# A fused attention and mixture-of-experts layer: another order of attention work, and bias table and count moved to the last experts

## The chip, the cores and the metric

The kernel runs on one core of a Trainium2 chip. The metric is the device time of one execution in microseconds (us). All arithmetic on data is in 32-bit floats, in parts of the attention as a sum of a rounded high part and a low part.

## The reference, cut to what matters

```
mod = split(silu(c) @ w_ada + b_ada, 6)
h   = modulate(rms_norm(x), mod[0], mod[1])            # hc likewise from the context
out_a = windowed_gqa(qa, ka, va, ka_c, va_c, sink)     # 8 heads, scores, softmax, values
out_b = mla_latent(qn, qr, kn, kr, vb, ...)            # 8 heads, scores, softmax, values
y   = concat(out_a, out_b) @ w_o
x   = x + mod[2] * rms_norm(y)
h2  = modulate(rms_norm(x), mod[3], mod[4])
logits = h2 @ w_router + b_router;  top 4 of 32, softmax of the four
for each expert e: f += weight * (swiglu(h2 @ w_gate_up[e] + b_gate_up[e]) @ w_down[e] + b_down[e])
x   = x + mod[5] * rms_norm(f)
```

There are 256 tokens and 256 context tokens of width 1024, 32 experts with an inner width of 1024.

## The kernel before

**Stages.** A first stage loads the first part of the ada weights, normalizes and projects. A second stage, the list of calls from line 751 on, does what is left of the keys and queries, the attention of both head groups, the output projection and the rest of the ada sums. A short stage after it (`XSEQ`) adds the residual, computes the router's logits and picks the experts. Then 32 experts run one after the other, and `finish` scales and writes the output. In the second stage and after it SP, PE, VectorE, ScalarE and GpSimd each run their instructions in the order of the program: the calls are a schedule written out by hand.

**Expert weights.** Each expert has 12 tiles of 128 x 2048 floats (1 MB each): 0 to 3 and 4 to 7 for the two halves of gate and up, 8 to 11 for down. `load` (line 730) sends them on SP's queue, each into one of 18 slots in the fixed order `RSEQ` (line 31): `d0` to `d2` are buffers of the projections, `r` the three buffers of the ring `slot`, `k0`, `q0`, `b0`, `k1`, `q1`, `b1` buffers of the latent keys and queries, `w` two wide buffers that the output weights use before, `x` four more. A slot is filled again when PE has used its tile.

**Ada sums.** The last four of the six parts of `mod` are not computed on PE. `ada_load` (line 410) loads two rows of weights into a tile; at the first tile of a part it also clears the sum on GpSimd and loads the bias. `ada_do` (line 421) adds the tile, scaled, to the part's sum with two VectorE instructions. `ada(1)` (line 742) loads the next tile, if one is left, and then sums the oldest tile. Twelve tiles go through the ring `slot`, which has three buffers; the first two are loaded ahead (lines 751 and 752), then `v_split` (line 561) takes the third buffer, and keeps it until `v_up(3)` (line 566) has used it. So the load of an `ada(1)` waits for the buffer, and SP, which issues it, with it. `spread1` (line 599) sums a part over the partitions with products by ones and multiplies it with a row of gains, `spread0` (line 594) fetches that row on ScalarE's queue, `column` (line 609) turns a part into columns.

**Attention.** `k_mid` and `k_flip` copy and transpose the latent keys of one tile of tokens, `q_up` and `q_flip` those of the queries, `v_up` makes the values. `top_b(h)` (line 631) computes a head's scores once to find its maxima; `shift(g)` (line 638) negates the maxima of a group, transposes them on PE and copies them out; `weights(u)` (line 660) computes two heads' scores again, transposed, and takes exponentials; `values(u)` (line 701) multiplies by the values and divides by the sums; `mix(k)` (line 720) adds a pair of heads' share of the output projection, with the weights that `load_wo` (line 580) has loaded.

**Experts.** In the loop of line 1146, `G_` does half of a gate-and-up product, `T_` transposes its result and computes the activation, `D_` half of the down product; `take` gathers the tokens of the next pair of experts, `place` makes the matrix that puts an expert's rows back, `scatter` adds them to four accumulators `acc`. `first(t)` (line 1073) starts these accumulators with the weighted `b_down` table, which line 1081 fetches on ScalarE's queue. `count` (line 1096) counts the experts with more than 64 tokens; the count is read after `finish`, and decides whether a loop for the rest runs.

Of the kernel before, what the change touches and what calls it, by code (L numbers as in the profile page):

```python
# [7 lines left out]
F32 = mybir.dt.float32  # L8
# [10 lines left out]
P = 128  # L19
D = 1024  # L20
KD = D // P
T = 256
NT = T // P
E = 32
# [46 lines left out]
def layer_kernel(ctx, tc, x, cx, cc, wadr, bada, grows, win0, winB, winC, winD, wuqa, wuqb, wukv, wo, wr, wexp, bgu, bgx, bdn, cols, rows, consts, out):  # L71
# [93 lines left out]
    def pmm(shape=(P, 512)):  # L165
        return ps.tile(list(shape), F32, name="mm", tag="mm", bufs=4)
# [240 lines left out]
    ada_n = [0]  # L407
# [119 lines left out]
    def k_mid(i):  # L527
        k96[i] = pqa.tile([P, 8, 96], F32, name="k96", tag="ct", bufs=2)
        S.copy(k96[i][:, :, 0:64], pk[i].rearrange("p (h d) -> p h d", h=8))
        S.copy(k96[i][:, :, 64:96], krt[:, i][:, None].to_broadcast([P, 8, 32]))  # L530

    def k_flip(i):
        for g in range(2):
            pt = ptp((96, 4, P))
            for j in range(4):
                PE.transpose(pt[:, j], k96[i][:, g * 4 + j], ident)
            ks = slice(i * P, (i + 1) * P)
            split(kTm[0][g][0:96, :, ks], kTm[1][g][0:96, :, ks], pt)
# [31 lines left out]
    y = []  # L570
# [9 lines left out]
    def load_wo(i):  # L580
        w = wide()
        nc.sync.dma_start(w, wo[i])
        for k in range(2):
            wov[2 * i + k] = w[:, k * 1024:(k + 1) * 1024]
# [11 lines left out]
        S.dma_start(gs_[ch], bass.AP(tensor=grows.tensor, offset=grows.offset + (0 if ch == 0 else 1) * D,  # L596
                                             ap=[[0, P], [1, D]]))

    def spread1(ch):
        a, gs = accs[ch], gs_[ch]  # L600
        for n in range(2):
            sl = slice(n * 512, (n + 1) * 512)
            p_ = pmm((P, 512))
            PE.matmul(p_, ones_f, a[:, sl], start=True, stop=True)
            V.tensor_tensor(a[:, sl], p_, gs[:, sl], op=ALU.mult)
# [29 lines left out]
            PE.matmul(s_, qTm[n][0:96, 0, t, j], kTm[0][n][0:96, j], start=True, stop=True)  # L635
            V.tensor_reduce(mxs[n][:, t, j:j + 1], s_, axis=AX.X, op=ALU.max)

    def shift(g):

        m = mxs[g]  # L640
        if g == "a":
            m4 = m.rearrange("p t (h c) -> p t h c", h=2)[:, :, :, 0:4]
            V.scalar_tensor_tensor(m4, m4, -1.0, nsink.rearrange("p (h j) -> p h j", h=2)[:, None].to_broadcast([P, NT, 2, 4]),
                                   op0=ALU.mult, op1=ALU.min)
        else:
            V.tensor_scalar(m[:, :, 0:4], m[:, :, 0:4], -1.0, None, op0=ALU.mult)
        p_ = pmm((P, T))
        for t in range(NT):
            PE.transpose(p_[:, t * P:(t + 1) * P], m[:, t], ident)
        r = rows_[g] = av.tile([P, T], F32R, name="nmax", tag="nmax", bufs=2)  # L650
        S.copy(r, p_)
        if g == "a":
            for h in range(2):
                ess[h] = av.tile([P, T], F32, name=f"es{h}")
                S.activation(ess[h], r.bitcast(F32), AF.Exp, scale=A_SCALE, bias=col[:, G_SINK + h:G_SINK + h + 1])
# [4 lines left out]
    def weights(u):  # L660

        a = u < 4
        pT_[u] = [av.tile([P, 4, T], F32, name="pT", bufs=4) for h in range(2)]
        for g in range(2):
            st = [pmm((P, 2, T)) for h in range(2)]
            for kk in range(2):
                kt = 2 * g + kk
                ks = slice(kt * P, (kt + 1) * P)
                ops = []
                for h in range(2):  # L670
                    if a:
                        k_ = [x_[HALF[h], ks] for x_ in kTg]
                        q_ = [x_[HALF[h], :, u] for x_ in qTg]
                        sl, r = sel[HALF[h], u], rows_["a"][HALF[h]]
                    else:
                        n, j = divmod(2 * (u - 4) + h, 4)
                        k_ = [x_[n][0:96, j, ks] for x_ in kTm]
                        q_ = [qTm[n][0:96, i, :, j] for i in range(2)]
                        sl, r = sel[0:96, j], rows_[n][0:96]
                    ops.append([(k_[0], q_[0]), (k_[0], q_[1]), (k_[1], q_[0]), (sl, r)])  # L680
                for i in range(4):
                    for h in range(2):
                        PE.matmul(st[h][:, kk], *ops[h][i], start=(kk == 0 and i == 0), stop=(i == 3 and not (a and g)),
                                  skip_group_check=True)
                if a and g:
                    t = 3 - kt
                    for c in range(2):
                        for h in range(2):
                            PE.matmul(st[h][:, kk, t * P + c * 64:t * P + c * 64 + 64], mask_s[HALF[h], t, c],
                                      ident_b[HALF[h], HALF[h]], start=False, stop=True, skip_group_check=True)  # L690
            for h in range(2):
                S.activation(pT_[u][h][:, 2 * g:2 * g + 2], st[h], AF.Exp, scale=A_SCALE if a else B_SCALE)  # L692
        adds(u)
# [36 lines left out]
    def load(e, js):  # L730
        for j in js:
            q = RSEQ[len(slots) % len(RSEQ)]
            if q in "rw":
                w = slot() if q == "r" else wide()
            elif q == "x":
                w = rings2[0].tile([P, 2048], F32, name="slot2", tag="slot2")
            else:
                w = (cst if q in tag else p2).tile([P, 2048], F32, name="slot2", tag=tag.get(q, q))
            slots[e, j] = w
            nc.sync.dma_start(w, wexp[e * SLOTS + j])  # L740

    def ada(n):
        for _ in range(n):
            if ada_n[0] < 16:
                ada_load()
            if ada_q:
                ada_do()
# [4 lines left out]
    ada_load()  # L752
    v_split()
    k_mid(2)
    k_mid(3)
    shift("a")
    weights(0)
    k_flip(2)
    k_mid(0)
    weights(1)  # L760
    k_flip(3)
    k_mid(1)
    values(0)
    k_flip(0)
    q_up(0, 0)
    v_up(0)
    ada(1)
# [16 lines left out]
    load_wo(0)  # L784
    q_flip(1, 1)
    load_wo(1)
    ada(1)
    load(0, range(0, 3))
    top_b(0)
    open_y()  # L790
    mix(0)
    values(3)
    top_b(1)
    spread0(0)
    top_b(2)
    top_b(3)
    ada(1)
    mix(1)
    load_wo(2)
    shift(0)  # L800
    top_b(4)
    top_b(5)
    mix(2)
    column(1)
    weights(4)
    ada(1)
    top_b(6)
    top_b(7)
    mix(3)
    load_wo(3)  # L810
    ada(1)
    router_bias()
    spread1(0)
    shift(1)
    weights(5)
    ada(1)
    values(4)
# [1 line left out]
    weights(6)  # L819
    mix(4)  # L820
    ada(1)
    column(2)
    values(5)
    spread0(3)
    ada(1)
    load(0, range(3, 6))
    weights(7)
    mix(5)
    ada(1)
    values(6)  # L830
    load(0, range(6, 8))
    load(1, range(0, 1))
    ada(1)
    mix(6)
    assert ada_n[0] == 16 and not ada_q
    values(7)
    spread1(3)
    mix(KD - 1)
    st2.close()
    stB.close()  # L840
# [204 lines left out]
        V.tensor_tensor(sg, zg, sg, op=ALU.mult)  # L1045
        V.scalar_tensor_tensor(actT[:, 4 * c:4 * c + 4], zl, 1.0, sg, op0=ALU.add, op1=ALU.mult)  # L1046

    def scatter(y, ctt, last=False):
        for t in range(NT):
            for n in range(2):  # L1050
                PE.matmul(acc[t][n], ctt[HALF[n], t], y[HALF[n]], start=False, stop=last, skip_group_check=True)  # L1051

    def act_tile():
        return mo.tile([P, KD, CAP], F32, name="actT")
# [14 lines left out]
        g, i = gs2[e]  # L1069
        return lambda k: g.x[:, k, i]  # L1070

    def first(t):
        px = px_tile().rearrange("p k c -> p (k c)")
        PE.transpose(px[0:E, 0:P], wtok[t], ident)
        wT = mo.tile([E, P], F32, name="wT")
        V.tensor_copy(wT, px[0:E, 0:P])
        for n in range(2):
            PE.matmul(acc[t][n], wT, bd[:, n * 512:(n + 1) * 512], start=True, stop=False, skip_group_check=True)

    bd = mo.tile([E, D], F32, name="bd", tag="xg")  # L1080
    S.dma_start(bd, bdn)
    g0 = pre(0, V, oh0)
    pxs = [acc[0][g].rearrange("p (k c) -> p k c", c=P) for g in range(2)]
    for g in range(2):
# [58 lines left out]
    for e in range(E):  # L1143
        loads(12 * e + 12)
        nxt = e + 1 < E
        if e == 0:
            G_(0, 1, LOW)
            T_(0, 0)
            G_(0, 1, HIGH)
            G_(1, 0, LOW)  # L1150
            T_(0, 1)
            G_(1, 0, HIGH)
            D_(0, LOW)
            T_(1, 0)
            D_(0, HIGH)
            for i in range(2):
                g0.place(i)
            for t in range(NT):
                first(t)
            count()  # L1160
            continue
        g = gs2[e][0] if e % 2 == 0 else pre((e + 1) // 2) if nxt else None
        step = [g.place, g.place] if e % 2 == 0 else [g.take, g.take] if nxt else None
        if step:
            step[0](0)
        G_(e, 1, LOW)
        if step:
            step[1](1)
        if e:
            scatter(ys.pop(e - 1), gs2[e - 1][0].ctt[gs2[e - 1][1]])  # L1170
        G_(e, 1, HIGH)
        if nxt:
            G_(e + 1, 0, LOW)
        T_(e, 1)
        if nxt:
            G_(e + 1, 0, HIGH)
        D_(e, LOW)
        if nxt:
            T_(e + 1, 0)
        D_(e, HIGH)  # L1180
    scatter(ys.pop(E - 1), gs2[E - 1][0].ctt[1], True)

    def finish():
        ssy = [sm.tile([P, 2], F32, name="ssy") for t in range(NT)]
# [186 lines left out]
```

## Time and profile before

| | |
|---|---|
| three runs | 1194.08, 1198.37, 1199.73 us (median 1198.37) |
| profiled execution | 1202.73 us, span 1200.9 us, mean granted clock 0.978 |
| PE busy | 1108.5 us, 92% of the span |
| VectorE, ScalarE, GpSimd busy | 304.6, 231.9, 129.9 us |
| DMA | 446.58 MB, mean 372 GB/s |

The span runs from the first to the last instruction of the profiled execution. PE's busy time counts products that are stretched by waits and by a lower clock, so 92% does not say that PE is the limit. SPq and ACTq are the queues on which SP and ScalarE issue transfers; a transfer's issue is an instruction, its landing comes later. A mean over the span mixes stages: the DMA engines are idle in parts of the attention and never in the experts.

### The profile page before, as it was taken

To read this page: it belongs to the slowest core of one execution; us is meant where nothing else is said; L and a number is where in the kernel's file an instruction comes from. 1 tells how busy PE (TensorE), PEld (TensorE's weight loads), DVE (VectorE), ACT (ScalarE), POOL (GpSimd) and SP (SyncE) were. 2 spreads that over 40 slices of the span, in tenths; PEclk is the share of its full clock that TensorE was granted. 3 is DMA by queue.
4 is the path that set the end of the run, shared out by engine and by line. 5 is a ranking of instruction groups with operands and counts; after the bars stand their busy time and mean duration, and the time that the engine had idled before them with its cause. 6 is when DMAs were issued, how large, how long until landed. Compare 5 with 4: busy or idle time off the path is not lost. (4 is left out here: it accounts for less than half of the span.)

```text
span 1200.9 us, 13600 instructions
## 1 busy us (share of the span) xinstructions
PE 1108.5 (92%) x5441; PEld 476.4 (40%) x5441; DVE 304.6 (25%) x651; ACT 231.9 (19%) x509; POOL 129.9 (11%) x186
## 2 busy tenths in 40 slices
PE   7699999999999999999999899999998999999885
PEld 2588756553343434343333333333333333333321
DVE  3876566742111121211111111111111111111112
ACT  3533612131111111121111111111111111111101
POOL 0301313310101010101101010101010101010000
PEclk9889998998999999999999999999999999999998
DMA  9740182899999999999999999999999999999994
GB/s 379 289 163 31 36 352 103 324 412 422 419 421 420 421 419 420 419 420 420 421 420 421 420 420 421 420 421 420 420 420 421 420 420 420 421 420 421 420 421 176
DMA packets 63194, 446.58 MB, mean 372 GB/s; under 512 B 7284, under 2 KB 7540, under 8 KB 10008
## 3 DMA queue, kind: packets, MB, share of 16 engines
q1 hardware_dynamic: 62648, 444.24, 89.7%
q10 hardware_dynamic: 480, 1.44, 0.4%
q8 instruction: 44, 0.72, 0.2%
q14 instruction: 22, 0.18, 0.0%
HBM read 444.60 MB, written 1.05 MB: 371 GB/s over the span
## 5 line engine op out<-in xcount | busy, mean ns | idle before, releaser
L1021 PE MATMUL pw<-slot,xg 128*64 128x512 f32 x2048 | 467.5, 598 | 21.0 <-DMA slot<-in_wexp 21.0
L1021 PE MATMUL pw<-slot,actT 128*64 128x512 f32 x1024 | 242.8, 601 | 29.2 <-DMA slot<-in_wexp 28.0
L1021 PEld LDWEIGHTS pw<-slot,xg 128*64 128x64 f32 x2048 | 136.6, 136 | 303.4 <-issue 237.4
L1039 DVE TENSOR_TENSOR z<-pf,bg 128x512 f32<-128x512 f32 x64 | 44.3, 692 | 756.8 <-PE pf L1034 756.8
L1021 PEld LDWEIGHTS pw<-slot,actT 128*64 128x64 f32 x1024 | 68.6, 136 | 179.6 <-issue 103.3
L1043 ACT ACTIVATE sg<-z 128x256 f32<-128x256 f32 x64 | 26.7, 417 | 312.2 <-DVE z L1041 312.2
L1028 ACT COPY gu<-pw 128x512 f32<-128x512 f32 x64 | 37.5, 586 | 229.4 <-PE pw L1021 229.4
L988 PEld LDWEIGHTS px<-oh,xt 128*128 128x128 f32 x480 | 57.2, 195 | 23.9 <-issue 23.9
L1051 PE MATMUL acc<-y,ctt 64*128 64x512 f32 x256 | 63.6, 615 | 0.7 <-ACT y L1028 0.7
L988 PE MATMUL px<-oh,xt 128*128 128x128 f32 x480 | 62.9, 285 | 0.3 <-DVE cnt L1106 0.3
L1000 ACT ACTIVATE xg<-px,vcol 128x128 f32<-128x128 f32 x120 | 45.2, 457 | 92.0 <-PE px L988 92.0
L1034 PEld LDWEIGHTS pf<-con,gu 128*128 128x128 f32 x256 | 26.8, 140 | 52.7 <-issue 51.1
L1034 PE MATMUL pf<-con,gu 128*128 128x128 f32 x256 | 42.0, 286 | 0.7 <-ACT gu L1028 0.7
L1028 ACT COPY y<-pw 128x512 f32<-128x512 f32 x32 | 18.8, 587 | 92.6 <-PE pw L1021 92.6
L723 PE MATMUL y<-slot,of 128*128 128x512 f32 x64 | 32.4, 651 | 2.5 <-DVE of L718 2.3
L978 POOL TENSOR_SCALAR oh<-con,posm,r 128x64 f32<-128x64 f32 x60 | 34.0, 586 | 2.5 <-DVE posm L918 2.5
L1045 DVE TENSOR_TENSOR sg<-z,sg 128x256 f32<-128x256 f32 x64 | 27.2, 425 | 18.0 <-ACT sg L1043 18.0
L1051 PEld LDWEIGHTS acc<-y,ctt 64*128 64x128 f32 x256 | 22.0, 186 | 21.8 <-issue 18.4
L698 POOL TENSOR_TENSOR pa<-pT 128x512 f32<-128x512 f32 x16 | 21.6, 1348 | 70.7 <-ACT pT L692 59.9
L1046 DVE SCALAR_TENSOR_TENSOR actT<-z,sg 128x256 f32<-128x256 f32 x64 | 27.2, 425 | 2.2
L274 PE MATMUL mm<-slot,siluz 128*4 128x512 f32 x40 | 20.0, 653 | 7.5 <-DMA slot<-in_wadr 7.5
L124 POOL TENSOR_TENSOR rstd<-rstd,mh 128x1 f32<-128x1 f32 x14 | 10.7, 766 | 136.9 <-DVE rstd L121 132.9
(449 smaller groups left out, 874.0 us busy)
## 6 DMA issues: line engine op xcount, KB each, us to landing
slot<-in_wexp SPq DMA_DIRECT2D x384, 1024.0 KB, 19.9
slot<-in_wadr SPq DMA_DIRECT2D x20, 1024.0 KB, 8.4
ax<-in_wadr SPq DMA_DIRECT2D x4, 1024.0 KB, 5.8
slot<-in_wo SPq DMA_DIRECT2D x4, 1024.0 KB, 4.8
slot<-in_win SPq DMA_DIRECT2D x2, 1024.0 KB, 8.5
slot<-in_winD SPq DMA_DIRECT2D x2, 768.0 KB, 9.7
slot<-in_winB SPq DMA_DIRECT2D x2, 576.0 KB, 4.8
ct<-in_cx SPq DMA_DIRECT2D x2, 512.0 KB, 8.5
```

The source lines that it names most:

```text
L723: PE.matmul(y[t][n], oT[k][:, t * P:(t + 1) * P], wov[k][:, n * 512:(n + 1) * 512], start=(k == 0), stop=(k == KD - 1), skip_group_check=True)
L978: eng.tensor_scalar(oh[t][:, i], iota[:, 0:CAP], pos_ap(t), r2[t], op0=ALU.is_equal, op1=ALU.mult)
L988: PE.matmul(px[:, k, 0:ne * CAP], xt[t][:, kk * P:(kk + 1) * P], self.oh[t][:, 0:ne].rearrange("p e c -> p (e c)"), start=(k == 0 and t == ...
L1000: S.activation(o, i, AF.Identity, scale=vcol[:, 1, kk:kk + 1], bias=vcol[:, 0, kk:kk + 1])
L1021: PE.matmul(pt[HALF[h]], lhs(k), wk(k, h), start=(k == 0), stop=(k == KD - 1), skip_group_check=True)
L1028: S.copy(y, pt)
L1034: PE.transpose(pf[:, b].rearrange("p h c -> p (h c)"), gu[:, b * P:(b + 1) * P], ident)
L1039: V.tensor_tensor(z, pf, bias[:, :, :, None].to_broadcast([P, 4, 2, CAP]), op=ALU.add)
L1043: S.activation(sg, zg, AF.Sigmoid, scale=ALPHA)
L1045: V.tensor_tensor(sg, zg, sg, op=ALU.mult)
L1046: V.scalar_tensor_tensor(actT[:, 4 * c:4 * c + 4], zl, 1.0, sg, op0=ALU.add, op1=ALU.mult)
L1051: PE.matmul(acc[t][n], ctt[HALF[n], t], y[HALF[n]], start=False, stop=last, skip_group_check=True)
```

## The change

The order of calls in the second stage is altered, and two pieces of the expert stage move.

- The negation of the maxima becomes a function of its own, `negate(g)`, called ahead of `shift(g)`. The first `negate` and `shift` come ahead of `k_mid(3)`, and `k_flip(2)` ahead of `weights(0)`.
- Of the twelve `ada(1)`, two move up to places ahead of `weights(0)` and `weights(1)`, and the last four end behind `values(5)` instead of behind `values(6)`; an assertion that all are done moves with them.
- `values(0)` goes behind `k_flip(0)`; `values(3)` behind `mix(0)` and `top_b(1)`; `mix(1)` ahead of `spread0(0)` and `top_b(2)`; `column(2)` behind the last sum; `values(7)` ahead of `mix(6)`. `spread1(3)` is split into its two halves, ahead of `values(7)` and of `mix(7)`.
- In the experts, the two `place` of expert 0 stand ahead of the two halves of its down product. `first` is split into `bias_rows`, `bias_flip` and `bias_add` and moves into expert 30; the first `scatter` starts the accumulators instead. `count` moves into expert 29.

```
     ada_load()
     v_split()
     k_mid(2)
+    negate("a")
+    shift("a")
     k_mid(3)
-    shift("a")
+    k_flip(2)
+    ada(1)
     weights(0)
-    k_flip(2)
     k_mid(0)
+    ada(1)
     weights(1)
     k_flip(3)
     k_mid(1)
+    k_flip(0)
     values(0)
-    k_flip(0)
     q_up(0, 0)
     v_up(0)
     ada(1)
...
     load_wo(1)
-    ada(1)
-    load(0, range(0, 3))
     top_b(0)
     open_y()
     mix(0)
+    top_b(1)
+    ada(1)
+    load(0, range(0, 3))
     values(3)
-    top_b(1)
+    mix(1)
+    load_wo(2)
     spread0(0)
     top_b(2)
     top_b(3)
+    negate(0)
     ada(1)
-    mix(1)
-    load_wo(2)
+    column(1)
+    mix(2)
     shift(0)
     top_b(4)
     top_b(5)
-    mix(2)
-    column(1)
+    ada(1)
     weights(4)
-    ada(1)
     top_b(6)
     top_b(7)
+    negate(1)
     mix(3)
     load_wo(3)
-    ada(1)
     router_bias()
     spread1(0)
     shift(1)
+    ada(1)
     weights(5)
...
-    column(2)
     values(5)
     spread0(3)
     ada(1)
+    column(2)
     load(0, range(3, 6))
     weights(7)
     mix(5)
-    ada(1)
     values(6)
     load(0, range(6, 8))
     load(1, range(0, 1))
-    ada(1)
+    spread1(3, (0,))
+    values(7)
     mix(6)
-    values(7)
-    spread1(3)
+    spread1(3, (1,))
     mix(KD - 1)
...
             G_(1, 0, HIGH)
+            g0.place(0)
             D_(0, LOW)
             T_(1, 0)
+            g0.place(1)
             D_(0, HIGH)
-            for i in range(2):
-                g0.place(i)
-            for t in range(NT):
-                first(t)
-            count()
             continue
...
-            scatter(ys.pop(e - 1), gs2[e - 1][0].ctt[gs2[e - 1][1]])
+            scatter(ys.pop(e - 1), gs2[e - 1][0].ctt[gs2[e - 1][1]], e == 1)
         G_(e, 1, HIGH)
+        if e == E - 3:
+            count()
+        if e == E - 2:
+            bd = bias_rows()
+            for t in range(NT):
+                bias_flip(t)
         if nxt:
             G_(e + 1, 0, LOW)
+        if e == E - 2:
+            for t in range(NT):
+                bias_add(t, bd)
         T_(e, 1)
```

## Rows read from the trace of the kernel before

**Rows 1.** Stretches: busy PE, PEld, DVE, ACT, POOL; granted clock, DMA share, GB/s

```profile
235.00:1186.00 951.00, 896.78 (x4268) 334.34 (x4268) 150.68 (x394) 149.11 (x340) 72.07 (x124) 0.99 1.01 418
...
182.00:195.00 13.00, 13.00 (x42) 8.57 (x41) 9.16 (x10) 2.17 (x4) 4.80 (x4) 0.61 0.00 0
...
288.00:298.00 10.00, 9.05 (x23) 4.30 (x22) 1.27 (x7) 0.00 (x0) 0.00 (x0) 0.52 1.01 422
```

**Rows 2.** Waits of SP's queue: total us, times, longest

```profile
SPq L740 <- DMA slot<-in_wexp: 698.0, 332, 8.6
...
SPq L418 <- PE pr L148: 0.2, 1, 0.2
```

**Rows 3.** Timeline of PE, last tile: start, us, operation, idle before it

```profile
1185.53 1.94 PE L1021 MATMUL pw<-slot,actT 128*64 128x512 f32 x8 [0.44 <-DMA slot<-in_wexp]
```

**Rows 4.** Timeline of SP's queue in the attention

```profile
158.54 0.33 SPq L418 DMA_DIRECT2D slot<-in_wadr  x1
...
230.65 2.50 SPq L740 DMA_DIRECT2D slot<-in_wexp  x5
```

**Rows 5.** Timeline of VectorE in the attention

```profile
125.80 1.28 DVE L138 TENSOR_TENSOR kTl<-tp,kTm 96x512 fp32r<-96x512 f32 x2 [5.73 <-ACT kTm L137]
...
228.03 2.60 DVE L431 SCALAR_TENSOR_TENSOR vpost<-slot,silu,vpost 128x1024 f32<-128x1024 f32 x2
```

**Rows 6.** Transfers by issue: queue, times, KB each, median us to landing

```profile
slot<-in_wexp SPq DMA_DIRECT2D x384, 1024.0 KB, 19.9
...
slot<-in_wo SPq DMA_DIRECT2D x4, 1024.0 KB, 4.8
...
bd<-in_bdn ACTq DMA_DIRECT2D x1, 128.0 KB, 7.9
```

**Rows 7.** Landing of L740's tiles, issued from 255 to 260, then 308.6

```profile
DMA to landing us min/median/max: 13.8/13.8/13.8
...
DMA to landing us min/median/max: 7.0/7.0/7.0
```

**Rows 8.** Landing of L418's tile issued at 158.5

```profile
DMA to landing us min/median/max: 5.9/5.9/5.9
```

**Rows 9.** Timeline of PE in the attention

```profile
128.46 1.95 PE L707 MATMUL mm<-pT,vg 128*64 128x256 f32 x16
...
131.20 0.97 PE L536 MATMUL tp<-con,k 128*96 128x128 f32 x7
...
158.71 0.71 PE L635 MATMUL mm<-kTm,qTm 96*128 96x512 f32 x2
159.26 3.98 PE L723 MATMUL y<-slot,of 128*128 128x512 f32 x8
...
188.63 5.71 PE L723 MATMUL y<-slot,of 128*128 128x512 f32 x8
...
211.47 1.84 PE L612 MATMUL mm<-con,accw 128*128 128x1 f32 x16
...
215.56 0.74 PE L683 MATMUL mm<-qTm,kTm 96*128 96x256 f32 x4
...
219.91 3.60 PE L723 MATMUL y<-slot,of 128*128 128x512 f32 x8
...
228.16 3.70 PE L723 MATMUL y<-slot,of 128*128 128x512 f32 x8 [2.35 <-DVE of L718]
...
235.93 3.60 PE L723 MATMUL y<-slot,of 128*128 128x512 f32 x8
```

**Rows 10.** Timeline of PE and VectorE in the first expert

```profile
281.25 3.65 PE L1021 MATMUL pw<-slot,actT 128*64 128x512 f32 x16
...
283.32 0.42 DVE L1046 SCALAR_TENSOR_TENSOR actT<-z,sg 128x256 f32<-128x256 f32 x1
...
286.82 0.28 PE L1074 MATMUL px<-con,wtok 128*32 128x128 f32 x1 [0.46 <-ACT ctt L1015]
...
295.80 3.40 PE L988 MATMUL px<-oh,xt 128*128 128x128 f32 x16 [0.33 <-DVE cnt L1106]
```

More of the change, by code (lines that the diff above doesn't have):

```diff
@@ L597, in spread0, with spread1 @@
                                              ap=[[0, P], [1, D]]))
-    def spread1(ch):
+    def spread1(ch, ns=(0, 1)):
         a, gs = accs[ch], gs_[ch]
-        for n in range(2):
+        for n in ns:
             sl = slice(n * 512, (n + 1) * 512)
@@ L636, in top_b, with negate @@
             V.tensor_reduce(mxs[n][:, t, j:j + 1], s_, axis=AX.X, op=ALU.max)
-    def shift(g):
+    def negate(g):
         m = mxs[g]
@@ L646, in shift @@
             V.tensor_scalar(m[:, :, 0:4], m[:, :, 0:4], -1.0, None, op0=ALU.mult)
+    def shift(g):
+        m = mxs[g]
         p_ = pmm((P, T))
@@ L754, in layer_kernel @@
     k_mid(2)
+    negate("a")
+    shift("a")
     k_mid(3)
-    shift("a")
+    k_flip(2)
+    ada(1)
     weights(0)
-    k_flip(2)
     k_mid(0)
+    ada(1)
     weights(1)
@@ L762, in layer_kernel @@
     k_mid(1)
+    k_flip(0)
     values(0)
-    k_flip(0)
     q_up(0, 0)
@@ L786, in layer_kernel @@
     load_wo(1)
-    ada(1)
-    load(0, range(0, 3))
     top_b(0)
@@ L791, in layer_kernel @@
     mix(0)
+    top_b(1)
+    ada(1)
+    load(0, range(0, 3))
     values(3)
-    top_b(1)
+    mix(1)
+    load_wo(2)
     spread0(0)
@@ L796, in layer_kernel @@
     top_b(3)
+    negate(0)
     ada(1)
-    mix(1)
-    load_wo(2)
+    column(1)
+    mix(2)
     shift(0)
@@ L802, in layer_kernel @@
     top_b(5)
-    mix(2)
-    column(1)
+    ada(1)
     weights(4)
-    ada(1)
     top_b(6)
     top_b(7)
+    negate(1)
     mix(3)
     load_wo(3)
-    ada(1)
     router_bias()
@@ L814, in layer_kernel @@
     shift(1)
+    ada(1)
     weights(5)
@@ L821, in layer_kernel @@
     ada(1)
-    column(2)
     values(5)
@@ L825, in layer_kernel @@
     ada(1)
+    assert ada_n[0] == 16 and not ada_q
+    column(2)
     load(0, range(3, 6))
@@ L828, in layer_kernel @@
     mix(5)
-    ada(1)
     values(6)
@@ L832, in layer_kernel @@
     load(1, range(0, 1))
-    ada(1)
+    spread1(3, (0,))
+    values(7)
     mix(6)
-    assert ada_n[0] == 16 and not ada_q
-    values(7)
-    spread1(3)
+    spread1(3, (1,))
     mix(KD - 1)
@@ L1046, in swiglu, with scatter @@
         V.scalar_tensor_tensor(actT[:, 4 * c:4 * c + 4], zl, 1.0, sg, op0=ALU.add, op1=ALU.mult)
-    def scatter(y, ctt, last=False):
+    def scatter(y, ctt, begin=False, last=False):
         for t in range(NT):
             for n in range(2):
-                PE.matmul(acc[t][n], ctt[HALF[n], t], y[HALF[n]], start=False, stop=last, skip_group_check=True)
+                PE.matmul(acc[t][n], ctt[HALF[n], t], y[HALF[n]], start=begin, stop=last, skip_group_check=True)
     def act_tile():
@@ L1070, in xcol, with bias_rows, bias_flip, bias_add @@
         return lambda k: g.x[:, k, i]
-    def first(t):
+    wTs = {}
+    def bias_rows():
+        bd = mo.tile([E, D], F32, name="bd", tag="xg")
+        S.dma_start(bd, bdn)
+        return bd
+    def bias_flip(t):
         px = px_tile().rearrange("p k c -> p (k c)")
         PE.transpose(px[0:E, 0:P], wtok[t], ident)
-        wT = mo.tile([E, P], F32, name="wT")
-        V.tensor_copy(wT, px[0:E, 0:P])
+        wTs[t] = mo.tile([E, P], F32, name="wT")
+        V.tensor_copy(wTs[t], px[0:E, 0:P])
+    def bias_add(t, bd):
         for n in range(2):
-            PE.matmul(acc[t][n], wT, bd[:, n * 512:(n + 1) * 512], start=True, stop=False, skip_group_check=True)
-    bd = mo.tile([E, D], F32, name="bd", tag="xg")
-    S.dma_start(bd, bdn)
+            PE.matmul(acc[t][n], wTs[t], bd[:, n * 512:(n + 1) * 512], start=False, stop=False, skip_group_check=True)
     g0 = pre(0, V, oh0)
@@ L1152, in layer_kernel @@
             G_(1, 0, HIGH)
+            g0.place(0)
             D_(0, LOW)
             T_(1, 0)
+            g0.place(1)
             D_(0, HIGH)
[L1156 to L1160, printed above, removed]
             continue
@@ L1169, in layer_kernel @@
         if e:
-            scatter(ys.pop(e - 1), gs2[e - 1][0].ctt[gs2[e - 1][1]])
+            scatter(ys.pop(e - 1), gs2[e - 1][0].ctt[gs2[e - 1][1]], e == 1)
         G_(e, 1, HIGH)
+        if e == E - 3:
+            count()
+        if e == E - 2:
+            bd = bias_rows()
+            for t in range(NT):
+                bias_flip(t)
         if nxt:
             G_(e + 1, 0, LOW)
+        if e == E - 2:
+            for t in range(NT):
+                bias_add(t, bd)
         T_(e, 1)
@@ L1180, in layer_kernel @@
         D_(e, HIGH)
-    scatter(ys.pop(E - 1), gs2[E - 1][0].ctt[1], True)
+    scatter(ys.pop(E - 1), gs2[E - 1][0].ctt[1], last=True)
     def finish():
```

## The prediction

> **What bounds the kernel now.** I read the stretches first. From 235 to 1186 us the DMA share is 1.01 at 418 GB/s, while PE has 54 us of idle time in them [rows 1]. The SP queue's waits are, by far, waits for earlier expert tiles to land [rows 2], and the last products still wait 0.44 us for the last tile, 15.4 us before the span ends [rows 3]. So the end is set by one stream: 384 expert tiles of 1.05 MB, 2.5 us each at that rate, some 960 us, then a tail of 15 us that is the same in both kernels. Only two things move it: when the stream becomes continuous, and whether it later runs dry because PE has not emptied a slot (18 slots; the order is that of `RSEQ`).
>
> It becomes continuous at 230.65, when SP sends the sixth tile and four more in one burst [rows 4]. That tile waits for a ring slot that the twelfth ada sum still reads; the sum ends at 228.03 + 2.60 = 230.63 [rows 5]. Then the stream is held by PE at two places, seen from issue to landing. A tile sent alone lands after 4.8 us [rows 6]. The first slot refilled after an expert product (257.0) landed 13.8 us after its issue, so PE could be 9.0 us later relative to the stream before a gap opens. The tile sent at 308.6 took 7.0, which leaves 2.2 us [rows 7]: it follows a stretch from 288 to 301 in which PE freed no slot, because it worked through token places, bias table and count.
>
> **The change part by part.** I number the twelve ada calls of the main order A1 to A12, and the tiles that they sum #1 to #12 (#1 and #2 are loaded ahead).
>
> *The end of the sums.* A12 stood behind values(6); now it stands right behind values(5). That is what lets the stream start earlier.
>
> *SP's order.* A1 and A2 move ahead of weights(0) and weights(1), so what was A3 moves up behind v_up(0). Its load, #5, needs the third ring slot, which v_split holds until v_up(3) has read it. In the kernel before, #5 was sent at 158.54 [rows 4], and SP had waited for that very product, 0.2 us [rows 2]; nothing was queued behind it but tiles not yet due. Now #5 and #6 stand ahead of load_wo(0) and load_wo(1) on SP, so both output weights wait for v_up(3), and mix(0), which follows it closely on PE, waits for load_wo(0) to land. Price: a lone tile 4.8, two tiles ahead of it 5.0, and the share of the gain rows sent by ACT at the same moment, which made #5 take 5.9 for 4.8 [rows 6, 8], 1.1: together 10.9 us after #5's issue.
>
> *values(0) behind k_flip(0).* values(0) took 2.74 us (128.46 to 131.20) and ran ahead of k_flip(0) [rows 9], whose buffers come free only with the copies of k_flip(3). Those stay behind the exponentials of weights(1). Bounds 0 and 2.74; I take 2.1, near the upper end, because ACT's list of work up to there is the same. The earlier negation and shift save nothing here, since ACT has the same copies to make before the first exponentials; A1 and A2 cost nothing, because VectorE waits 5.73 us for ACT there [rows 5]. So #5 goes out at 158.54 + 2.1 = 160.6 and mix(0) starts at 171.5, against 159.26 [rows 9]: 12.2 us later.
>
> *From mix(0) to the end of mix(7).* Before: 159.26 to 239.53, 80.3 us. The work at full clock, by rows [rows 9]: eight mix at 3.60, 28.8; five values at 2.74, 13.7; four weights at 4.35 (215.56 to 219.91), 17.4; seven maxima at 0.55, 3.9; two columns at 1.84, 3.7; both spreads, costed like columns, 3.7; transposes and the router's bias about 1. Sum 72.2; the other 8.1 us were half clock and waits for VectorE (2.35 us before mix(6) alone). The new order removes most of those waits: A5 and later ones fall beside products, values(6) and values(7) are apart from the mix that needs them. Where VectorE's sums come to stand late I cost them at nothing, since PE covers them; without that cover each is 2.60 [rows 5]. But PE has idled for 10 us, and a mix in a stretch at mostly half clock (mean 0.61, so largely 1.2 of 2.4 GHz) took 5.71 for 3.60 [rows 1, 9]: I add 2.1 for mix(0). So mix(7) ends at 171.5 + 72.2 + 2.1 = 245.8, 6.3 us later than before. A12: up to values(5) the same list gives 47.8 (five mix, three values, three weights, the maxima, one column, one spread), plus 2.1, plus 2.35 until the reciprocal is done, plus 2.6: 226.3, 4.3 us earlier than 230.63.
>
> *The ring.* PE 6.3 later and the stream 4.3 earlier makes 10.6 of relative shift, against 9.0 of slack at the first refill: 1.6 us are lost there, and the stream ends 6.3 - 9.0 = -2.7 us. What follows mix(7) up to the first expert product is untouched.
>
> *Bias table and count.* They ran on PE from 286.82 to 295.80 [rows 10], 9.0 us at a mean clock of 0.52 [rows 1], with nothing to cover them. Removing them gives PE 9.0; the token places, now between products, cost back about 2.5: place(1) stands behind T_(1,0), whose last VectorE step ends at 283.74, while the next product could start at 281.25 [rows 10]. Bounds 0 and 3.0. With 6.5 gained the second narrow place allows 6.3 - 6.5 - 2.2 = -2.4 us. This part therefore shortens nothing by itself; without it the second place would eat the gain.
>
> *At the end.* Count goes to expert 29, where PE waits for tiles anyway: nothing; without that cover about 1 us. In expert 30 the bias rows are fetched late, and four products wait for them behind G_(31,0,LOW). They took 7.9 us to land [rows 6], with the tile queue full. Two tiles at 2.50 pass meanwhile, so PE loses about 2 and spends 1.9 on the products; 14 tiles (35 us) are left, in which it needs 14 x 1.94 = 27 [rows 3] and some 4 for transposes and the scatter. I take 0.5 for what remains at the end, bounds 0 and 3.
>
> A rule weighed here: the Trainium skill, "DMA: Bandwidth & Descriptors", section "Queues, rings and completion order", says that each DMA engine takes turns packet by packet between the queues that have work. By that rule the rows from ACT's queue pass the eight tiles of SP's queue; the 7.9 us beside tiles that took 19.9 in the median [rows 6] agree. If they did not, PE would lose some 12 us there, of which about 8 would reach the end.
>
> Sum: -2.7 + 0.5, about -2 us. The profiled execution took 1202.7 (its span and 1.8 around it), so the sum gives 1200.5 for it; it is 4.3 above the median of 1198.4, and I take the same difference off that. Forecast 1196, its own range 1191 to 1203.
>
> **Rivals.** *wo not late (1184).* If load_wo(0) landed in time, by a free slot or another order on SP, mix(0) would start at 161.4 and stay warm: PE 6.3 - 10.1 - 2.1 = -5.9, the stream -14.9 at the first refill, -14 in all. For it: the DMA engines stand idle from 182 to 195 [rows 1], so an earlier stream has room. Against: SP's wait on v_up(3) is in the trace, and SP keeps its order.
>
> *Half clock (1205, slower).* Place: PE from mix(0) on, after its 10 us wait. A stretch at half clock adds 0.59 of its work. The trace has one from 182 to 195 with PE busy throughout [rows 1], so it need not end with mix(0). The end moves with PE once the ring binds, so it is slower than before from a PE delay of 9, and by 0.5% from 15: 14 us of work at half clock beyond what I counted. The skill's "TensorE: Matmul & The Clock Gate" (section "Why this matters for your kernels") warns of just such idle gaps between bursts; the trace's own row is the reason for the chance.
>
> *Nothing gained (1199).* The sums end earlier, but the ring gives it all back: relative shift 10.6 rather than 9.0 with PE 9 later. For it: both narrow places are within 2 us of my sum.
>
> **How the numbers follow.** About 0.5% (6 us) is what a measurement of this kernel can tell from no change. Forecast 0.58, wo not late 0.12, half clock 0.16, nothing gained 0.14. Of the forecast's share 0.15 lies better than 1192.4 (fewer waits, less than 2.1 for values(0)) and 0.02 beyond 1204.4. Faster 0.12 + 0.15 = 0.27, slower 0.16 + 0.02 = 0.18, same 0.55. The range goes from 1184, the first rival, to 1204, between nothing and the second.
>
> **What would show it.** Right: SP sends load_wo(0) at about 161.5, PE is idle for some 10 us ahead of mix(0) and then at half clock; the sixth expert tile goes out at 225 to 228; landing times at the first refill of an expert slot fall to 5 or 6 us; no stretch without issues around 290 to 300. Wrong: load_wo(0) sent near 152; PE reaching its first expert product earlier than before; a DMA share below 1 later than 300; PE waiting for the bias rows longer than 5 us.

## The result, and the profile of the changed kernel

| | median, us | range, us |
|---|---|---|
| before | 1198.26 | 1194.08 to 1199.73 |
| changed | 1215.69 | 1213.67 to 1215.98 |

The changed kernel takes 1.0148 times as long, with an interval of 1.012 to 1.0175. The forecast of 1196 us had the wrong sign, and the time lies above its range. The profiled execution took 1215.98 us, 0.3 above the median; that of the kernel before was 4.5 above its own, so gains read between these two traces are some 4 us too large.

The end of the kernel shows it. First the waits of PE (us in total, times, longest us) and of SP's queue:

```profile
PE acc L1094 <- DMA bd<-in_bdn: 21.0, 1, 21.0
PE tp L536 <- DVE kTl L138: 4.3, 1, 4.3
```

```profile
SPq L743 <- DMA slot<-in_wexp: 658.5, 316, 3.0
...
SPq L418 <- PE pr L148: 5.7, 1, 5.7
```

L1094 is `bias_add`, the product with the bias rows: PE stood still for 21 us ahead of it. SP waits for tiles 658.5 us, which were 698.0 [rows 2]; but it waits 658.6 us in `bd_early` below, which has no such stall, so this sum does not tell where the loss is. (L536 and L418 are taken up below.) The timelines of ScalarE and of PE around it:

```profile
1136.07 0.59 ACT L1035 COPY gu<-pw 128x512 f32<-128x512 f32 x1 [5.19 <-PE pw L1028]
1155.74 0.34 ACTq L1083 DMA_DIRECT2D bd<-in_bdn  x1
```

```profile
1161.43 7.19 PE L1094 MATMUL acc<-bd,wT 32*128 32x512 f32 x8 [21.00 <-DMA bd<-in_bdn]
1168.55 1.11 PE L1041 MATMUL pf<-con,gu 128*128 128x128 f32 x4
1169.59 6.17 PE L1028 MATMUL pw<-slot,xg 128*64 128x512 f32 x16
...
1201.45 1.99 PE L1058 MATMUL acc<-y,ctt 64*128 64x512 f32 x8 [0.74 <-ACT y L1035]
```

ScalarE finished its copy at 1136.66 and had only the fetch of the bias rows to issue; it issued it 19.1 us later. The rows then landed in 5.6 us. The stretches (columns as in [rows 1]) show what PE did when they came, and that the stream was done long before the end:

```profile
1140.00:1145.00 5.00, 0.43 (x2) 0.00 (x0) 0.00 (x0) 0.00 (x0) 0.00 (x0) 0.90 1.01 419
...
1155.00:1160.00 5.00, 0.00 (x0) 0.00 (x0) 0.00 (x0) 0.00 (x0) 0.00 (x0) 0.50 1.02 403
...
1165.00:1170.00 5.00, 5.00 (x11) 1.99 (x11) 0.30 (x1) 0.00 (x0) 0.00 (x0) 0.50 0.80 334
1170.00:1175.00 5.00, 5.00 (x14) 1.33 (x12) 1.73 (x5) 0.42 (x1) 0.00 (x0) 0.53 0.30 123
```

The granted clock fell to 0.50 (1.2 GHz) while PE stood still and was still there when it worked again: the eight products took 7.19 us, and 16 gate-and-up products 6.17 where [rows 10] show 3.65 for 16. The last expert tile landed in the stretch with the DMA share of 0.30, near 1173, some 12 us earlier than the 1185.5 of [rows 3] by the two traces. But the last scatter ended at 1203.4. The stream no longer set the end; PE did.

In the attention, SP's queue answers [rows 4], VectorE and PE answer [rows 5, 9]:

```profile
140.61 13.61 SPq L418 DMA_DIRECT2D slot<-in_wadr  x2
154.65 1.01 SPq L582 DMA_DIRECT2D slot<-in_wo  x2
161.46 0.33 SPq L418 DMA_DIRECT2D slot<-in_wadr  x1
161.83 1.60 SPq L743 DMA_DIRECT2D slot<-in_wexp  x3
```

```profile
121.36 7.38 DVE L431 SCALAR_TENSOR_TENSOR accw<-slot,silu,accw 128x1024 f32<-128x1024 f32 x4
128.67 1.27 DVE L138 TENSOR_TENSOR kTl<-tp,kTm 96x512 fp32r<-96x512 f32 x2
...
210.93 2.60 DVE L431 SCALAR_TENSOR_TENSOR vpost<-slot,silu,vpost 128x1024 f32<-128x1024 f32 x2
```

```profile
129.40 1.53 PE L536 MATMUL tp<-con,k 128*96 128x128 f32 x8 [4.35 <-DVE kTl L138]
...
162.17 3.98 PE L726 MATMUL y<-slot,of 128*128 128x512 f32 x8
...
231.46 3.60 PE L726 MATMUL y<-slot,of 128*128 128x512 f32 x8
```

Both output weights were sent at 154.65, not 161.5 or later; mix(0) began at 162.17, 2.9 us later than before; mix(7) ended at 235.06, 4.5 earlier; the twelfth sum ended at 213.53, 17.1 earlier. These are differences between two traces as they stand, and the two executions were already 3.9 us apart ahead of the first altered call. The same copies of a mask on VectorE show it, first before, then changed:

```profile
118.92 1.16 DVE L522 COPY mask_s<-mask_b 64x256 bf16<-64x256 bf16 x4 [0.88 <-PE mm L148]
114.99 1.16 DVE L522 COPY mask_s<-mask_b 64x256 bf16<-64x256 bf16 x4 [0.88 <-PE mm L148]
```

Counted from there, mix(0) is 6.8 us later than before, mix(7) ends 0.5 earlier, and the twelfth sum ends 13.2 earlier. `exp_only` below, with the old order of attention and these copies at 115.28, has mix(0) at 155.62, the end of mix(7) at 234.92 and that of the sum at 224.31: against it the changed kernel is 6.6 later, 0.1 later and 10.8 earlier. So PE gains nothing up to the end of mix(7); what gains, by 11 to 13 us, is the end of the sums.

### The profile page after: what moved, and what is told of

Its sections match the earlier page's. It is cut to its first block, busy times and chain, and to the rows that moved or that the text cites. A ratio compares the mean times of both kernels' runs of the same rounds, so it can differ in the third digit from the quotient of the medians.

```text
span 1214.2 us, 13597 instructions
## 1 busy us (share of the span) xinstructions
PE 1107.7 (91%) x5441; PEld 474.7 (39%) x5441; DVE 306.0 (25%) x651; ACT 231.6 (19%) x509; POOL 131.7 (11%) x186
## 4 chain that ended last, share of the span: by engine, by line
DMA 64%; PE 30%; DVE 4%; ACT 1%; issue 1%; POOL 0%; SPq 0%; POOLq 0%; DVEq 0%; ACTq 0%
DMA slot<-in_wexp 63%; PE pw L1028 11%; PE y L726 2%; PE mm L686 2%; PE mm L274 2%; PE mm L710 1%; PE mm L148 1%; PE mm L146 1%; PE mm L147 1%; PE acc L1058 1%; DVE accw L431 1%; PE px L995 1%; PE pr L547 1%; PE pf L1041 1%; PE acc L1094 1%
## 5 line engine op out<-in xcount | busy, mean ns | idle before, releaser
L1094 PE MATMUL acc<-bd,wT 32*128 32x512 f32 x8 | 7.2, 1072 | 21.0 <-DMA bd<-in_bdn 21.0
## 6 DMA issues: line engine op xcount, KB each, us to landing
slot<-in_wexp SPq DMA_DIRECT2D x384, 1024.0 KB, 19.9
ct<-in_cx SPq DMA_DIRECT2D x2, 512.0 KB, 10.9
```

## The experiments

Theory S: the gain of the attention is there, and what hides it is the late issue of the bias rows. The rivals of S put the 23 us into the late adds and flips themselves, into the shared buffer (`tag="xg"`), or into the order of packets between the two queues. "Ratio" is to the kernel before on the same chip, 95% intervals in brackets. Four chips were used: the kernel before took 1196.76 us beside `bd_early`, `att_only`, `exp_only` and `bd_own_late`, 1197.62 beside `bd_pool_late`, `bd_at20`, `exp_early` and `early_place_old`, 1198.6 beside `early_sums_later`, `early_v0_first` and `early_sums_later_place_old`, and 1197.3 beside `early_both`.

**The two halves, and the bias rows early.** `bd_early`: everything of the change, but the rows are fetched where the kernel before fetches them, into a buffer of their own.

```diff
-        bd = mo.tile([E, D], F32, name="bd", tag="xg")
+        bd = mo.tile([E, D], F32, name="bd", bufs=1)
...
+    bd = bias_rows()
     g0 = pre(0, V, oh0)
...
-            bd = bias_rows()
             for t in range(NT):
                 bias_flip(t)
```

> The changed kernel, with the bias rows in a buffer of their own and fetched where the kernel before fetched them, ahead of the first expert. Theory A (the loss is the late fetch of the bias rows): PE has no wait of 21 us in expert 30 any more, the end follows the last expert tile, which landed at about 1173 in the changed kernel, by the old tail of 15.4: 1189 of span, about 1190 us, faster than before by some 8. Rival B (the attention order itself costs): 1205 or more.

1192.15 us, ratio 0.9963 [0.995, 0.9975]: faster than both kernels, and some 2 us above the 1190 that was expected. Its bias rows by tile (ns min/median/max, first and last start), and PE's last tile:

```profile
L1094 PE MATMUL acc<-bd,wT x8: 587/587/692, 1141.4 to 1144.5; 32*128 32x512 f32 x8
L1083 ACTq DMA_DIRECT2D bd<-in_bdn x1: 387/387/387, 247.9 to 247.9; - x1
```

```profile
1175.09 1.94 PE L1028 MATMUL pw<-slot,actT 128*64 128x512 f32 x8 [0.43 <-DMA slot<-in_wexp]
1177.77 1.99 PE L1058 MATMUL acc<-y,ctt 64*128 64x512 f32 x8 [0.74 <-ACT y L1035]
```

The adds, at the same late place, wait for nothing and run at full clock, and the last product waits 0.43 us for its tile, as in [rows 3]. Against it the 23.7 us between the two last scatters (1203.44 and 1179.76) split: the adds start 20.0 us later (1161.43, 1141.4) and last 3.5 longer (7.19 against 3.7). What follows takes 34.7 us there and 34.8 in the changed kernel, in the one because the tiles come no faster, in the other because PE works through it, at first at half clock, and makes nothing good.

The next three take one half of the change's diff each. `att_only`: experts of before, attention of the change. `exp_only`: attention of before, experts of the change. `exp_early`: that one with the rows fetched early.

> Only the attention part of the change, the experts as before. Theory A: no late bias rows, so no loss at the end; the stream starts as early as in the changed kernel, but the bias table and count are back in expert 0, where the kernel before had only 2.2 us left: of the 12 us by which the stream ended earlier, about 7 go there, 1193 us. Without that second narrow place: 1186 to 1190. Rival B: 1205 or more.

> Only the expert part of the change, the attention in the order of before. Theory A: the stream ends where it ended before (about 1185), but the bias rows are sent some 19 us late in expert 30 and PE works some 35 us behind them: 1220 to 1227 us, slower than the whole change. Rival B (the attention order costs, the late rows are hidden): 1199 to 1201.

> The kernel before's attention, with the changed experts and the bias rows fetched early into a buffer of their own (count, flips and adds in the last experts, places between the down products). Theory of the prediction (the early work taken out of the first experts is worth something only to a stream that starts earlier): the same as before within 0.4 %, ratio 0.997 to 1.001, since the second narrow place had slack in the kernel before. Rival (the 4.6 us of bd_early come from the experts' part alone): ratio 0.994 to 0.997.

| | experts before | experts changed, rows early | experts changed, rows late |
|---|---|---|---|
| attention before | 1 | 0.9996 [0.9985, 1.0007] | 1.0208 [1.0183, 1.0233] |
| attention changed | 1.0025 [1.0012, 1.0038] | 0.9963 [0.995, 0.9975] | 1.0148 [1.012, 1.0175] |

Neither half gains anything alone, and the attention's costs 0.25%; together they gain 0.37%. `exp_only` issued the rows at 1160.7, and PE waited 21.2 us. Where the attention's gain went without the experts' part, the stretches of `att_only` show:

```profile
284.00:288.00 4.00, 3.63 (x6) 1.05 (x5) 0.97 (x5) 0.00 (x0) 0.00 (x0) 0.50 1.01 422
...
292.00:296.00 4.00, 3.96 (x18) 3.77 (x20) 0.00 (x0) 0.17 (x1) 0.00 (x0) 0.50 0.63 258
296.00:300.00 4.00, 4.00 (x16) 1.05 (x14) 0.00 (x0) 1.34 (x4) 0.00 (x0) 0.79 0.22 29
300.00:304.00 4.00, 4.00 (x26) 2.55 (x24) 0.00 (x0) 1.51 (x4) 0.00 (x0) 1.00 0.86 297
304.00:308.00 4.00, 4.00 (x20) 1.35 (x20) 0.00 (x0) 0.08 (x1) 0.00 (x0) 1.00 0.67 231
```

Behind bias table and count, which still ran there at half clock, the DMA engines idled 6.5 us (four times 0.37 + 0.78 + 0.14 + 0.33). In `bd_early` these stretches are full. The 1193 us expected of `att_only` (it took 1198.42) counted on a stream that ended 12 us earlier; 3.9 of these are the difference between the two executions told above.

**What held the issue.** `bd_own_late` keeps the late place but gives the rows their own buffer. `bd_pool_late` does that too, and issues them on GpSimd's queue. `bd_at20` issues them on ScalarE, with their own buffer, in expert 20. The edits of the two, on top of `bd_own_late`:

```diff
-        S.dma_start(bd, bdn)
+        G.dma_start(bd, bdn)
```

```diff
+        if e == 20:
+            bd = bias_rows()
         if e == E - 2:
-            bd = bias_rows()
```

> The changed kernel with the bias rows in a buffer of their own, fetched at the same late place. Theory A1 (the issue on ACT waits for a completion semaphore that it shares with the expert tiles on SP's queue, until a tile sent just ahead has landed): nothing changes, about 1215, and the rows are again sent some 19 us after the evict of expert 30. Rival A2 (it waits for the buffer that it shares with the gathered tokens): sent at once, PE waits 3 us at most, about 1192.

> The changed kernel, with the bias rows fetched at the same late place (expert 14 of 16 by the code's own test e == E - 2 counted from the last) into a buffer of their own, but issued by GpSimd instead of ScalarE. Theory S (a completion semaphore that the bias rows' transfer shares with the expert tiles holds the issue back): the GpSimd issue shares none with SP's tiles, it is not held, the rows land some 6 to 10 us after the evict before them, PE waits under 2 us for them and the time is that of bd_early, 1192 us (1189 to 1196). Rival R (the rows land late because their packets take turns with the tiles in flight, whichever engine issues them): PE waits some 20 us again and the time is 1213 to 1217 us.

(The "expert 14 of 16" in it is a slip: the place is expert 30 of 32.)

> The changed kernel, with the bias rows fetched in expert 20 on ScalarE's queue into a buffer of their own; flips, adds and count stay late. Theory S: ScalarE's issue is held up to 20 us there as well, and PE waits for the evict behind it in the middle of the stream; an expert leaves PE some 2.4 us of slack, so the lost time is made good within ten experts, nothing waits for the rows at the end, and the time is 1192 to 1197 us. Rival C (the cost of 23 us lies in the adds and flips late in the last experts, not in the wait for the rows): 1212 to 1217 us. Rival T (every us that PE loses to the held queue stays lost, because the ring is held full behind it and the stream stops): some 1204 to 1212 us.

`bd_own_late`: a single run, 1215.28 us; the rows were issued at 1156.4 and PE waited 20.8, so the buffer is not it. `bd_pool_late`: 1193.07, ratio 0.9967 [0.9952, 0.9982]. GpSimd issued the fetch as soon as it stood there, and it took 6.1 us to land beside the full tile queue:

```profile
1125.55 0.60 POOL L1019 TENSOR_SCALAR wo__6474<-oh,wtr 128x128 f32<-128x128 f32 x1
1126.10 0.72 POOL L1083 DMA_DIRECT2D bd<-in_bdn  x1
```

GpSimd comes to the fetch 10 us earlier than ScalarE did, which accounts for little of the gain: 6.1 us from 1136.7 would end at 1142.8, 2.6 us after the adds began here (1140.2). So neither the place in the code, nor the packets' turns, nor the late adds cost the time; the wait ahead of the issue does.

What the issue waits for stands in the program. Every transfer that SP or ScalarE issues counts its landing on one of eight completion semaphores, which the program takes in turn, and ScalarE's fetch takes its place in the same turn: it waits until the transfer that had its semaphore last has landed. GpSimd's fetch has a semaphore of its own and waits for none. The semaphore events of the traces show the fetch and the tile that shares its semaphore (times in us):

| | tile issued by SP | its last part on the semaphore | rows issued by ScalarE |
|---|---|---|---|
| changed | 1135.86 | 1155.72 | 1155.74 |
| `exp_only` | 1140.87 | 1160.70 | 1160.73 |
| `bd_own_late` | 1136.51 | 1156.35 | 1156.37 |
| `bd_at20` | 840.19 | 860.17 | 860.19 |
| before | 233.72 | 251.84 | 251.86 |

The rows leave 0.02 us after the tile's last part has landed, each time. A tile in the full stream takes 20 us to land, because SP's tiles take the same turn: up to eight are on their way, at 2.5 us each. In `bd_at20`, the rows of that tile and of ScalarE, what PE waited for, and the stretches:

```profile
L743 SPq DMA_DIRECT2D slot<-in_wexp x1: 327/327/327, 840.2 to 840.2; - x1
...
who waited for it (us, times):
  ACT sg L1050: 24.4, 1
...
DMA to landing us min/median/max: 20.0/20.0/20.0
```

```profile
860.19 0.34 ACTq L1083 DMA_DIRECT2D bd<-in_bdn  x1
860.58 0.42 ACT L1050 ACTIVATE sg<-z 128x256 f32<-128x256 f32 x1 [24.36 <-DMA slot<-in_wexp]
```

```profile
PE pf L1041 <- ACT gu L1035: 12.5, 2, 11.8
```

```profile
850.00:860.00 10.00, 0.00 (x0) 0.00 (x0) 0.00 (x0) 0.00 (x0) 0.00 (x0) 0.70 1.01 420
860.00:870.00 10.00, 8.48 (x32) 3.68 (x33) 2.88 (x7) 1.89 (x4) 0.00 (x0) 0.62 1.02 404
870.00:880.00 10.00, 10.00 (x57) 4.86 (x57) 0.00 (x0) 3.01 (x8) 0.00 (x0) 1.00 1.01 419
```

`bd_at20` took 1193.45, ratio 0.9963 [0.9947, 0.998]. ScalarE was held 24 us, and PE, which first had other products to do, stood 11.8 us for the copy behind the fetch. The stream never stopped (DMA share 1.01 or 1.02), and with eleven experts left PE caught up: this stall cost nothing. The stall of 21 us two experts from the end cost 22.

**The smaller terms.** All on top of `bd_early`. `early_place_old` puts both `place` of expert 0 behind the down products again.

```diff
-            g0.place(0)
             D_(0, LOW)
             T_(1, 0)
-            g0.place(1)
             D_(0, HIGH)
+            for i in range(2):
+                g0.place(i)
```

> bd_early (changed attention, bias rows early), with the two token places again behind both down products, as before. Theory P (the second narrow place eats the gain unless the first group of the second expert starts early, and the places are part of that, PE 2.4 us of work against an idle stretch): the tile landings at 292 to 308 us dip again and the time lies 1 to 4 us above bd_early's, 1193 to 1196. Rival N (the places' move is worth nothing, since the bias and the count, over 8 us of PE and VectorE work, are what gave the room): within 0.8 us of bd_early, 1191.3 to 1193.

1192.39, ratio 0.9952 [0.9934, 0.9969]: the move of the places is worth nothing that these runs can tell. In the changed kernel it makes PE wait 2.8 us for VectorE at L1021, and that wait is gone here. So the room in the first experts comes from the bias table and the count; the two were not tried apart.

`early_sums_later`: the two ada sums that stand ahead of k_flip(3) go behind k_flip(0) and q_up(0, 0), each with the load of the next tile that its call makes. `early_v0_first`: values(0) ahead of k_flip(0). `early_both`: both. `early_sums_later_place_old`: the sums and the places.

```diff
     k_flip(2)
-    ada(1)
     weights(0)
     k_mid(0)
-    ada(1)
...
     k_flip(0)
+    ada(1)
     values(0)
     q_up(0, 0)
+    ada(1)
```

```diff
-    k_flip(0)
     values(0)
+    k_flip(0)
```

> The changed kernel with the bias rows fetched early (the kernel of bd_early), and the two ada sums that the change put ahead of the split of k_flip(3) put behind k_flip(0) and behind q_up(0, 0). Theory D (the 4.3 us that k_flip(0)'s flips wait for that split are VectorE's 7.4 us of sums, and PE carries nearly 3 us of it on to mix(7)): no such wait, mix(0) and mix(7) some 3 us earlier, the idle stretch of the stream at the first refill (some 3.5 us) shorter by as much; time 2 to 3 us under bd_early, 1189 to 1191, if the expert stream starts no later. Rival L (the two sums gate SP's next ada loads and by them the stream): the stream starts as many us later as PE gains, so no gain, 1192 to 1196.

> The kernel of bd_early with values(0) ahead of k_flip(0), as in the kernel before; nothing else changed. The prediction's term: values(0) behind k_flip(0) costs PE 2.1 us; undone, it gives up to 2.1 us less of an idle stretch at the first refill, 1190 to 1191.5. Rival: VectorE is held by the two sums in either order, values(0) only fills PE's 4.3 us of idle time in front of the k_flip(0) flips, so PE gains all of 2 to 4 us up to mix(7): 1188.5 to 1190.5. Rival 2: the stream does not see it, 1192.

> The kernel of early_sums_later with values(0) ahead of k_flip(0): both edits of the attention's start on top of the early bias rows. Theory F (both edits remove the same wait, PE's at k_flip(0) for VectorE's split): what is left of it in early_sums_later is 1.5 us, so at most 1.5 us more is gained up to mix(7), and the first refill, whose idle time there is already under 2 us, gives at most that: ratio to the kernel before 0.991 to 0.9935, 1188 to 1190.5 by its 1198.6. Rival A (the two are independent and add): ratio near 0.990, some 1186.5.

> Both edits on bd_early: the two sums later, and the two token places behind both down products as before. If the two edits are independent the time is that of early_sums_later less 0 to 1 us, since the old place of the token places measured 1192.4 against 1192.2 to 1193.4 for the new one. If instead the places' move is needed once PE runs earlier, it is 1 to 3 us above early_sums_later.

| | median, us | ratio |
|---|---|---|
| early_sums_later | 1189.96 | 0.9932 [0.9913, 0.9951] |
| early_v0_first | 1190.68 | 0.9935 [0.9917, 0.9953] |
| early_both | 1190.33 | 0.9938 [0.991, 0.9965] |
| early_sums_later_place_old | 1192.54 | 0.9939 [0.9911, 0.9967] |

PE at k_flip(0) and at its last tile in `early_sums_later`, then the stretches in which the stream idles most, in `bd_early` and in `early_sums_later`:

```profile
130.02 1.24 PE L536 MATMUL tp<-con,k 128*96 128x128 f32 x8 [1.47 <-DVE kTl L138]
...
1170.07 1.94 PE L1028 MATMUL pw<-slot,actT 128*64 128x512 f32 x8 [0.44 <-DMA slot<-in_wexp]
```

```profile
248.00:252.00 4.00, 3.60 (x32) 3.48 (x33) 1.77 (x7) 0.00 (x0) 1.75 (x3) 1.00 0.89 352
252.00:256.00 4.00, 4.00 (x21) 1.43 (x22) 1.53 (x8) 2.17 (x8) 0.00 (x0) 1.00 0.25 57
```

```profile
248.00:252.00 4.00, 4.00 (x21) 1.29 (x18) 2.06 (x10) 1.63 (x7) 0.00 (x0) 1.00 0.54 144
252.00:256.00 4.00, 4.00 (x22) 1.30 (x20) 0.73 (x4) 1.50 (x2) 0.00 (x0) 1.00 1.03 418
```

With the sums later, PE's wait for VectorE falls from 4.34 us (in `bd_early`) to 1.47, and the idle time of the stream from 236 to 256 falls from 4.7 to 1.8 us. mix(7) begins at 228.27 instead of 232.86 and the last product at 1170.07 instead of 1175.09; but the two executions differ by 2.8 us the other way ahead of the altered calls (the copies of the mask at 118.50 and 115.69), and the profiled one of `early_sums_later` was 2.7 us faster than its own median, so these starts do not give the size of the gain. In the medians it is 2 us, in the ratios some 3.7 (0.9963 to 0.9932, on different chips, with intervals that just touch): likely, but not clear of the noise. `early_both` gains nothing beyond either, as expected of two cures for one wait; its PE waits 2.8 us for VectorE's split a step later, at the flips of q (L556). The last of the four had the widest spread (1186.37 to 1193.87) and decides nothing. The version to keep is `early_sums_later` or `early_v0_first`, which these runs don't tell apart: by their ratios about 0.65% faster than before and 2% faster than the change.

## Why the prediction was wrong

**The step that failed is "At the end".** It took 7.9 us [rows 6] as the whole time from the place in the code to the rows in the buffer, but that number runs from the issue to the landing. The landing was sized on the safe side: 5.6 us. The 19.1 us ahead of it had no term, so the bounds of 0 and 3 did not contain the risk. The trace of before had its sign, which was not read. Its bias rows were held too, for one microsecond, behind the issue of another small table's fetch:

```profile
250.53 0.33 ACTq L964 DMA_DIRECT2D bg<-in_bgu  x1
251.86 0.34 ACTq L1081 DMA_DIRECT2D bd<-in_bdn  x1
```

ScalarE was free at 250.86 and issued the second at 251.86, when the tile with its semaphore, issued at 233.7, had landed after 18.1 us. There the stream had begun some 20 us earlier, so the tile was about to land; in the middle of the stream a tile has up to its whole 20 us ahead of it.

The rule of turns by packet (the Trainium skill, "DMA: Bandwidth & Descriptors", "Queues, rings and completion order") agrees with these traces: 5.6 and 6.1 us to landing beside tiles of 20. The other branch, rows behind the tiles, was put at some 12 us of which 8 reach the end. The loss came by a cause outside that rule, and was 21 us of waiting, 23.7 at the end. Of the 4 us that PE was to make good (35 us of tiles against 27 + 4 of work) 3 went to the half clock behind the adds (6.17 us for 3.65, and four transposes 1.11 for 0.66).

**"SP's order" failed as well, on the other side.** The fifth ada tile was said to need the buffer that v_split holds until v_up(3). It was sent at about 140.6, right behind the sum that frees another buffer (137.98 + 2.60), and the wait for v_up(3), now 5.7 us instead of the 0.2 of [rows 2], fell to the seventh tile, at 161.46, behind both output weights. So no weight held mix(0) for long, and the 10.9 us were never due. The step read one pairing of tile and buffer in the trace of before as fixed, while moving the sums changed the order in which buffers came free.

**"values(0) behind k_flip(0)" was too small.** It predicted 2.1, and mix(0) was 6.6 to 6.8 later, with no wait for a weight in it. The step let A1 and A2 cost nothing because VectorE waits there [rows 5]; but their two sums, 7.38 us on VectorE, stood in front of k_flip(3)'s split, and k_flip(0) waited 4.35 us for it. Another 1.8 us went to the clock behind that wait, 0.55 from 130 to 132 and 0.59 from 132 to 134: k_flip(0) took 1.53 us, which is 1.08 in `early_both`, and the first products of values(0) 3.29 for 1.95 [rows 9]. `early_sums_later` takes most of this wait away, and `early_v0_first` and `early_both` all of it, though the one then waits 2.0 us for GpSimd in values(0) and the other the 2.8 us told above.

**"From mix(0) to the end of mix(7)"**: 72.2 at full clock; measured 72.9 (162.17 to 235.06). The 2.1 for a cold PE were not due here, since there was no 10 us wait. **"The end of the sums"**: right direction, 11 to 13 us instead of 4.3, mostly because mix(0) was not 12.2 us late and PE not cold. On the clock of the trace of before, 3.9 us later, mix(0) began at 166.1 and the sums ended at 217.5: 5.4 (171.5 to 166.1) and 2.1 off 226.3 give 218.8.

**"The ring"** held. PE 4.5 earlier and the sums 17.1 earlier by the traces make 12.6 of relative shift (10.9 against `exp_only`), 3.6 over the slack of 9.0; the stream idled 4.7 us there in `bd_early`.

**"Bias table and count"** held best: "shortens nothing by itself" is the 0.9996 of `exp_early`, "without it the second place would eat the gain" the 1.0025 of `att_only`. The 2.5 us that the places cost on PE are there (2.8) and are hidden.

**The rivals.** The condition of "wo not late" came true. It gave 1184; with the bias rows early it was 1192, and 1190 with the sums moved back. By its own working the stream gains 14; between the traces of before and `bd_early` the last product starts 10.4 us earlier. Of these, 3.2 stand ahead of the first altered call (the copies of the mask at 118.92 and 115.69), and the runs' medians show 4.6. The rival had PE 5.9 us earlier at the end of mix(7), where PE is 0.5 earlier at most, for the wait at k_flip(0). Why the first stage of the profiled execution of before was late is open, and so is the rest. "Half clock" came for some us in the attention, and at the other end of the kernel, there as a part of the cost and not its cause. No rival had the wait of an issue; the only sign of it was the last line of "What would show it": PE waiting for the bias rows longer than 5 us.

## What to carry to other kernels

A transfer's time in the profile starts at its issue; when a fetch is moved into a full stream, look also for what its issue will wait for, on which engine, and put that wait into the sum at the landing time of what is already under way. A fetch without dependences belongs early, or on a queue whose issue waits for none of the stream's transfers, and a stall is priced by the slack that is left after it: a hold of 24 us, 11.8 of them on PE, cost nothing eleven experts from the end, and 21 on PE cost 22 two experts from it. Before starts are compared between two traces, look at work that the change leaves alone: here the two were 3.9 us apart ahead of it. When two parts of a change are each worth nothing, measure them together, since one can be the room that the other needs.

## What the runs showed of the hardware

- Transfers of SP and ScalarE share eight completion semaphores in turn in this program, so one tiny fetch of 128 KB on an idle engine stood 19.1 us (and 24 in `bd_at20`) until a tile of another engine's queue had landed. It was issued 0.02 us after that. GpSimd's queue stood outside of it: no wait, 6.1 us to land.
- Packets of the small queue were not held by the big one: 5.6 us to landing with tiles beside it that took 19.9.
- While PE stood still for 21 us its granted clock went to 0.50, and eight products that took 3.7 us from first to last in `bd_early` took 7.19.
